# A chunked mLSTM recurrence: norm's first step in front of the decays, chunk loads half a chunk sooner, gated heads' lower parts on GpSimd and heads spread out

## Chip, core and metric

The kernel runs on one NeuronCore of a Trainium2 chip. The metric is the device time of one execution in microseconds (us); a time given for a kernel is the median of several executions. The engines are TensorE (PE, with its weight loads listed apart as PEld), VectorE (DVE), ScalarE (ACT), GpSimd (POOL) and SyncE (SP). PE writes to PSUM banks, which DVE or ACT have to read before the bank can be used again. DMAs are issued here from the queues of SP and POOL. Each engine works through its own queue in order and waits at an instruction until the semaphores it names are reached.

## The reference, cut

The whole program is one inference step of a two-layer decoder: an mLSTM layer, then an attention layer, each followed by a SwiGLU feed-forward part. The change lies in the first layer, in the recurrence over chunks of tokens and the gating behind it:

```python
def mlstm_chunk(state, inp):
    C, n, m = state
    q, k, v, li, lf = inp
    b = jnp.cumsum(lf, axis=-1)
    dmat = jnp.where(causal, b[..., :, None] - b[..., None, :] + li[..., None, :], -jnp.inf)
    m_t = jnp.maximum(inter, jnp.max(dmat, axis=-1))
    s = jnp.einsum('bhtk,bhsk->bhts', q, k) * jnp.exp(dmat - m_t[..., None])
    num = w_inter[..., None] * jnp.einsum('bhtk,bhkv->bhtv', q, C) + jnp.einsum('bhts,bhsv->bhtv', s, v)
    h = num / jnp.maximum(jnp.abs(den), jnp.exp(-m_t))[..., None]
    ...
    C_new = w_c[..., None, None] * C + jnp.einsum('bhs,bhsk,bhsv->bhkv', w_g, k, v)

h = rmsnorm(h, mh_g)                       # over each head's 128 values
out = (h.reshape(B, T, HV) * jax.nn.sigmoid(og)) @ w_out
```

There are 8 heads with 64 key and 128 value columns, 1024 prompt tokens, 16 meta tokens, and 64 sample tokens (8 rows of 8). All data are float32.

## The kernel before

**Tokens.** The 1104 tokens are cut into nine chunks: chunk 0 has the 64 sample and 16 meta tokens, chunks 1 to 8 have 128 each. Three groups `t` of three chunks (`GRP`) make up 336, 384 and 384 columns. Float32 matmuls are made of three products of a rounded high part and a low part (`xh`, `xl`, `whi`, `wlo`): lines L206, L207 and L208. The low part is the value minus its high part.

**The recurrence** (`recurrence`) goes over the chunks; the order of PE, DVE, ACT and POOL in it is the order in which the Python code issues instructions. For chunk `i` it does the following.
- `chunk_load` (four DMAs on POOL's queue: queries and keys `qk`, the decay exponents `eb` as a broadcast, the carry weights `wb` in two halves). The tiles come from three sets, so the load of chunk i + 3 reuses those of chunk i.
- `decay_steps`: eight DVE instructions on `eb`, one a head (L1381), and one exponential on ACT (L1384).
- `chunk_scores`: the products of queries and keys on PE (`sps`, L1398), multiplied into `eb` on DVE (L1400).
- `chunk_keys`: the keys turned (`kps`, L1415) and weighted (`kw` L1417, `wb` L1419).
- `chunk_state`: the new state `C` (PE L1448, DVE L1452, and a multiply on POOL, L1455).
- `chunk_out`: two halves z = 0 and 1 of four heads, each with products with the values (`nps`, L1521) and with the state (L1488); DVE copies the denominators (`den`, L1472), ACT the values (L1480). ACT then makes the exponential of the chunk after next and squares the heads (L1542); in chunks 7 and 8 DVE squares every other head (L1539).

**Filling.** Between these, `f(n)` issues n steps of another job, the matmuls for the output gates (`gates_out`, L206 to L208 into `mmA`): 24 pieces, each eight steps of three matmuls into one of two PSUM banks. ACT empties a bank with a sigmoid into one of three staging tiles `stg` (L994), and POOL stores that to DRAM as `ogD` (L995). The exponential, the root and the sigmoid need different function tables on ACT, and a change shows as ACT_TABLE_LOAD.

**Norm.** After chunks 2, 5 and 8, `norm_heads` normalizes the group's three chunks. Its first step is five small DVE instructions (L1601 to L1605) and a root on ACT (L1606). Its next steps are a reciprocal, a multiply, and one large multiply on DVE for each chunk (L1608 to L1612). For the first two groups these steps are issued inside the next chunk: `next(norm, None)` in `after`, which runs between the two halves of `chunk_out`. So they fall into chunks 3 and 6.

**Heads.** From chunk 7 on the gate job is nearly at its end, and `g` gates finished heads in place of it: five in chunk 7 and five in chunk 8. For a head, `gate_head` turns three chunks' values on PE into a bank `ghps` that it shares with `mmA` (L1628). DVE multiplies it with gain and gate in place of the gate tile (`ogqk`, `ogeb`, L1629). Then `split` rounds to the high part `xh` on ACT (L284) and subtracts for the low part `xl` on DVE (L285). The gate columns are loaded from `ogD` by POOL (L1010) into places made of old `qk` and `eb` tiles; a place is reused once its head is done. The remaining heads are gated later, in the output projection, with other tiles (`ogc`).

**Behind it.** The output projection (`pops`, `mlp`) takes its weights, split already, from DRAM as `wo<-woD`, in pairs of a high and a low half on SP's queue (L547). They go into memory that the recurrence's pools leave, so each pair waits for what used that memory last. POOL loads the residual columns `vA<-hD` (L506).

Of the kernel before, what the change touches and what calls it, by code (L numbers as in the profile page):

```python
# [8 lines left out]
F32 = mybir.dt.float32  # L9
# [19 lines left out]
NT = len(TT)  # L29
# [887 lines left out]
def phase_a(self, vt):  # L917
# [6 lines left out]
    with ExitStack() as c3:  # L924
# [76 lines left out]
        def heads(pp, tag, op=None, some=None):  # L1001
# [11 lines left out]
            def gate(t):  # L1013
                if not left[t]:
                    return False
                while todo and (len(ready) < 3 if callable(op) else op):
                    ahead()
                if t < 0:
                    return False
                og = ready.pop(0)  # L1020
                self.gate_head(t, left[t].pop(0), v, og, pp, tag)
                if not callable(op):

                    used.append(og)
                    if len(used) > 1:
                        op.append(used.pop(0))
                return True
# [161 lines left out]
def recurrence(self, kp, rec, v, qkD, fill, gate):  # L1189
# [15 lines left out]
    with ExitStack() as cr, self.pool("recAp", bufs=2, space=PSUM) as pp:  # L1205
# [28 lines left out]
        with self.pool("rec2") as sets[2], self.pool("rec1", bufs=2) as rp, self.pool("rec3") as sets[0]:  # L1234
# [7 lines left out]
            gate = gate(places)  # L1242
            for i in range(1, NT):
                N2 = load(i + 2) if i + 2 < NT else None
# [13 lines left out]
                def after():  # L1258
                    if i + 1 < NT:
                        self.chunk_keys(i + 1, N, pp, tm)  # L1260
                    if N2:
                        self.chunk_decay(i + 2, N2, tm, cap)
                    next(norm, None)
                    g(2)
                    g(3)
                    g(2)
                    next(norm, None)

                self.chunk_out(i, R, rp, *args, den, ssq, g, exp=N2 and (lambda: N2["exp"]()),
                               then=(lambda: next(state, None)) if i == NT - 1 else None, between=between, after=after)  # L1270
# [18 lines left out]
                R, N = N, N2  # L1289
# [170 lines left out]
def chunk_out(self, i, R, rp, pp, kp, C, v, qkD, eD, wD, tm, den, ssq, f, sp=None, exp=None, then=None, between=None, after=None):  # L1460
# [8 lines left out]
    def done(ps, g, hs):  # L1469
# [21 lines left out]
    if i == 0:  # L1491
        for g, hs in enumerate(((0, 2), (4, 6), (1, 3), (5, 7))):
# [14 lines left out]
            done(ps, g, hs)  # L1507
    else:

        ps = None  # L1510
        for z in range(2):
# [11 lines left out]
            if z:  # L1523
                carried(ps, False)
            for a in range(2):
                done(ps[a], 2 * z + a, (4 * z + a, 4 * z + 2 + a))
            if z == 0:
                after()
        f(2)
# [89 lines left out]
def gate_head(self, t, h, v, og, pp, tag):  # L1619
# [11 lines left out]
    self.split(og[:, :n], yh[:, h, g0:g1], yl[:, h, g0:g1])  # L1631
# [1451 lines left out]
```

## Time and profile before

| | us |
| --- | --- |
| median of 3 runs | 2799.47 |
| lowest, highest run | 2796.45, 2800.47 |
| profiled execution | 2798.37 |
| its span (first to last instruction) | 2796.5 |
| busy: PE, PEld | 2736.1, 2635.6 |
| busy: DVE, ACT, POOL | 1786.7, 1169.0, 848.6 |
| mean granted TensorE clock (1 is full) | 0.996 |

The profile is of one execution. Its totals say which engine is busy; a view in order of time shows for each engine what it ran and what ended the idle time ahead of it; windows give the busy time of each engine and the granted clock in a stretch; a view by line gives the least, median and greatest duration of one kind of instruction. All times on that axis are us from the first instruction. The recurrence takes the stretch from about 215 to 411 us. Busy time of PE is modelled from pipelined matmuls, so 98% is not 98% of its peak.

### The profile page before, as it was taken

The page shows a single profiled execution, that of the slowest core. Times are in us where ns is not written, and L with a number is a line of the kernel's source. Part 1 is how long each engine was busy: PE and PEld are TensorE (multiplying, and loading weights), DVE is VectorE, ACT ScalarE, POOL GpSimd, SP SyncE. Part 2 cuts the span into 40 slices and gives each one's busy share as a digit, 9 for nine tenths or more (in the row PEclk, how much of TensorE's full clock was granted, in tenths as well). Part 3 has the DMA queues.
Part 4 walks back from the last instruction along what each step waited for, and adds up shares of the span by engine and source line. Part 5 has one row for each costly group of instructions (what it writes and reads, how often), then busy time and mean ns, then how long its engine had stood idle before and what let it go on. Part 6 is the DMA issues. An engine that isn't in the chain of part 4 may idle for free. (4 is left out here: it accounts for less than half of the span.)

```text
span 2796.5 us, 60483 instructions
## 1 busy us (share of the span) xinstructions
PE 2736.1 (98%) x23525; PEld 2635.6 (94%) x23525; DVE 1786.7 (64%) x4008; ACT 1169.0 (42%) x2291; POOL 848.6 (30%) x1304
## 2 busy tenths in 40 slices
PE   9999989999999999999999999999999999999998
PEld 8999979999999999999999888777999999999998
DVE  5633556888887666563455443777388888765656
ACT  5432553423323334443444444777343323323345
POOL 3142333133322332124453202544313223323211
PEclk9999999999999999999999999999999999999999
DMA  7666555345554375545453776443524555526556
GB/s 213 176 183 179 152 153 207 105 148 169 166 176 140 117 249 174 188 145 168 139 177 130 246 281 229 158 141 95 150 79 134 175 175 169 162 90 228 185 193 221
DMA packets 432400, 473.05 MB, mean 169 GB/s; under 512 B 37014, under 2 KB 358290, under 8 KB 431090
## 3 DMA queue, kind: packets, MB, share of 16 engines
q1 hardware_dynamic: 380546, 319.98, 37.1%
q0 software_dynamic: 44928, 143.00, 15.6%
q10 hardware_dynamic: 6640, 6.21, 0.7%
q8 instruction: 185, 3.03, 0.5%
q14 instruction: 101, 0.83, 0.1%
HBM read 322.24 MB, written 146.83 MB: 168 GB/s over the span
## 5 line engine op out<-in xcount | busy, mean ns | idle before, releaser
L1685 PE MATMUL m<-xh,slot 128*128 128x276 f32 (+1 forms) x2752 | 539.1, 289 | 2.0 <-ACT fs L1714 2.0
L1685 PEld LDWEIGHTS m<-xh,slot 128*128 128x128 f32 x2752 | 439.1, 188 | 4.4 <-ACT fs L1714 2.6
L1685 PE MATMUL m<-xl,slot 128*128 128x276 f32 (+1 forms) x1376 | 396.7, 288 | 0.0
L1685 PEld LDWEIGHTS m<-xl,slot 128*128 128x128 f32 x1376 | 259.0, 188 | 0.0
L206 PE MATMUL tmps<-slot,xh 128*128 128x256 f32 (+2 forms) x864 | 243.1, 281 | 0.0
L208 PE MATMUL tmps<-slot,xl 128*128 128x256 f32 (+2 forms) x864 | 240.6, 278 | 0.0
L207 PE MATMUL tmps<-slot,xh 128*128 128x256 f32 (+2 forms) x864 | 240.5, 278 | 0.0
L285 DVE TENSOR_TENSOR slot<-slot,slot 128x1024 fp32r<-128x1024 f32 x124 | 162.0, 1307 | 60.1 <-ACT slot L284 58.6
L284 ACT CAST slot<-slot 128x1024 fp32r<-128x1024 f32 x124 | 129.5, 1045 | 142.1 <-PE m L1685 111.4
L207 PEld LDWEIGHTS tmps<-slot,xh 128*128 128x128 f32 (+1 forms) x864 | 159.1, 184 | 0.1
L208 PEld LDWEIGHTS tmps<-slot,xl 128*128 128x128 f32 (+1 forms) x864 | 158.6, 184 | 0.0
L206 PEld LDWEIGHTS tmps<-slot,xh 128*128 128x128 f32 (+1 forms) x864 | 158.4, 183 | 0.2
L206 PE MATMUL mmA<-xh,whi 128*128 128x384 f32 (+1 forms) x384 | 134.2, 349 | 3.8 <-ACT stg L994 3.7
L208 PE MATMUL mmA<-xh,wlo 128*128 128x384 f32 (+1 forms) x384 | 128.4, 334 | 0.0
L207 PE MATMUL mmA<-xl,whi 128*128 128x384 f32 (+1 forms) x384 | 128.4, 334 | 0.0
L285 DVE TENSOR_TENSOR slot<-vA,slot 128x1024 fp32r<-128x1024 f32 (+1 forms) x59 | 82.2, 1396 | 32.7 <-ACT slot L284 31.5
L285 DVE TENSOR_TENSOR slot<-Ht,slot 128x1024 fp32r<-128x1024 f32 (+1 forms) x59 | 82.1, 1394 | 32.7 <-ACT slot L284 31.5
L284 ACT CAST slot<-vA 128x1024 fp32r<-128x1024 f32 (+1 forms) x59 | 60.8, 1035 | 95.5 <-PE m L1685 86.5
L1789 DVE TENSOR_TENSOR ws<-ws 128x128 f32<-128x128 f32 x264 | 94.8, 359 | 8.9
L284 ACT CAST slot<-Ht 128x1024 fp32r<-128x1024 f32 (+1 forms) x59 | 60.8, 1034 | 94.8 <-PE m L1685 86.3
L2905 ACT ACTIVATE s<-s,nb 128x272 f32<-128x272 f32 (+7 forms) x126 | 98.9, 786 | 0.0
L2940 ACT COPY th<-tp 128x768 f32<-128x768 f32 (+1 forms) x80 | 73.5, 920 | 53.8 <-PE tp L2932 30.4
(792 smaller groups left out, 8635.9 us busy)
## 6 DMA issues: line engine op xcount, KB each, us to landing
ws<-in_w_down SPq DMA_DIRECT2D x176, 128.0 KB, 2.7
sD<-ws SPq DMA_DIRECT2D x176, 128.0 KB, 2.0
slot<-sD SPq DMA_DIRECT2D x40, 512.0 KB, 4.2
slot<-in_w_gate_up SPq DMA_DIRECT2D x36, 512.0 KB, 4.0
kp<-in_cache_k SPq DMA_DIRECT2D x32, 512.0 KB, 6.0
vp<-in_cache_v SPq DMA_DIRECT2D x32, 512.0 KB, 6.1
vA<-in_w_gate_up SPq DMA_DIRECT2D x26, 512.0 KB, 4.0
Ht<-in_w_gate_up SPq DMA_DIRECT2D x26, 512.0 KB, 4.0
```

Source lines behind the costliest of these rows:

```text
L206: mm(ps, sh, mh, start=first, stop=False)
L207: mm(ps, sh, ml, start=False, stop=False)
L208: mm(ps, sl, mh, start=False, stop=last)
L284: self.nc.scalar.copy(hi, src)
L285: self.nc.vector.tensor_tensor(out=lo, in0=src, in1=hi.bitcast(F32), op=ALU.subtract)
L1685: nc.tensor.matmul(u.ps[h, b], w[p][:, k], x[q][:, k], start=first and k == i == 0, stop=k == 3 and i == 2, skip_group_check=True)
L1789: tt(out=o, in0=a, in1=b, op=ALU.subtract)
L2905: nc.scalar.activation(ss[z, u], ss[z, u], AF.Exp, bias=nb[:, z : z + 1], accum_out=sm[:, u, z : z + 1])
L2940: nc.scalar.copy(th.rearrange("p x z (u h q) -> p h (x z u) q", h=2, q=64)[:, :, :n], pt[:, :, :n])
```

## The change

It has four parts, all in the recurrence of the first layer:
- In `after`, norm's first step is issued ahead of the decays of chunk i + 2 (it was behind them).
- The load of chunk i + 3 is issued at the end of `chunk_out` of chunk i (`done`), ahead of the last four fill steps. It was issued at the beginning of chunk i + 1, behind those steps. The load of chunk 3 stays in front of the loop.
- `gate_head` takes a flag: the ten heads that are gated within the recurrence have their low part subtracted on POOL instead of DVE. The later heads keep DVE.
- In chunks 7 and 8 the third head moves from between the halves to the second half, between its products with the values and those with the state (`amid`).

```diff
@@ heads / gate
-                self.gate_head(t, left[t].pop(0), v, og, pp, tag)
+                self.gate_head(t, left[t].pop(0), v, og, pp, tag, not callable(op))
@@ recurrence
+            N2 = load(3)
             for i in range(1, NT):
-                N2 = load(i + 2) if i + 2 < NT else None
+                N3 = None
...
                 def after():
                     if i + 1 < NT:
                         self.chunk_keys(i + 1, N, pp, tm)
+                    next(norm, None)
                     if N2:
                         self.chunk_decay(i + 2, N2, tm, cap)
-                    next(norm, None)
                     g(2)
                     g(3)
-                    g(2)
+                    if i < 7:
+                        g(2)
                     next(norm, None)
 
+                def done():
+                    nonlocal N3
+                    if i + 3 < NT:
+                        N3 = load(i + 3)
+
                 self.chunk_out(i, R, rp, *args, den, ssq, g, exp=N2 and (lambda: N2["exp"]()),
-                               then=(lambda: next(state, None)) if i == NT - 1 else None, between=between, after=after)
+                               then=(lambda: next(state, None)) if i == NT - 1 else None, between=between, after=after, done=done,
+                               amid=(lambda: g(3)) if i > 6 else None)
...
-                R, N = N, N2
+                R, N, N2 = N, N2, N3
@@ chunk_out (its inner function done is now called leave)
             if z:
+                if amid:
+                    amid()
                 carried(ps, False)
...
             if z == 0:
                 after()
+        done()
         f(2)
         f(2)
@@ gate_head
-    self.split(og[:, :n], yh[:, h, g0:g1], yl[:, h, g0:g1])
+    hi, lo = yh[:, h, g0:g1], yl[:, h, g0:g1]
+    nc.scalar.copy(hi, og[:, :n])
+    (nc.gpsimd if ahead else nc.vector).tensor_tensor(out=lo, in0=og[:, :n], in1=hi.bitcast(F32), op=ALU.subtract)
```

Below are three places as they stand on the engines; a row is the line, the operation, and out<-in with the shape, and x8 means eight such in a row. Lines of the changed kernel are about ten higher.

DVE in chunk 6, before: `rd` and `fA` are norm's small tiles, and the eight instructions on `eb` are the decays of chunk 8.

```order
L1417 TENSOR_TENSOR kw_4338<-kps_4547,tmA 128x512
L1419 TENSOR_TENSOR wb_4337<-qk_4336,wb_4337 128x512
L1381 SCALAR_TENSOR_TENSOR eb_4486<-eb_4486,tmA,cap 128x128 x8
L1601 SCALAR_TENSOR_TENSOR rd_4562<-den 128x24
L1602 TENSOR_TENSOR rd_4562<-rd_4562,tmA 128x24
L1603 RECIPROCAL rd_4562<-rd_4562 128x24
L1604 TENSOR_TENSOR fA_4563<-ssqA,rd_4562 128x24
L1605 TENSOR_TENSOR fA_4563<-fA_4563,rd_4562 128x24
L1608 RECIPROCAL fA_4563<-fA_4563 128x24
```

The same place with the change:

```order
L1425 TENSOR_TENSOR kw_4300<-kps_4547,tmA 128x512
L1427 TENSOR_TENSOR wb_4299<-qk_4298,wb_4299 128x512
L1612 SCALAR_TENSOR_TENSOR rd_4554<-den 128x24
L1613 TENSOR_TENSOR rd_4554<-rd_4554,tmA 128x24
L1614 RECIPROCAL rd_4554<-rd_4554 128x24
L1615 TENSOR_TENSOR fA_4555<-ssqA,rd_4554 128x24
L1616 TENSOR_TENSOR fA_4555<-fA_4555,rd_4554 128x24
L1389 SCALAR_TENSOR_TENSOR eb_4453<-eb_4453,tmA,cap 128x128 x8
L1619 RECIPROCAL fA_4555<-fA_4555 128x24
```

The decays have moved between norm's first five instructions and its reciprocal, which waits for ACT's root.

POOL from chunk 5 to chunk 6, before: the last load of the loop, that of chunk 8, with the stores of gate columns around it.

```order
L995 DMA ogD<-stg_4416 128x384
L995 DMA ogD<-stg_4458 128x384
L1328 DMA qk_4485<-qkD 128x8x128
L1327 DMA eb_4486<-eD 128x8x128
L1332 DMA wb_4487<-wD 64x4x128 x2
L1455 TENSOR_TENSOR C_107<-C_105,wcP 128x516
```

The same place with the change:

```order
L995 DMA ogD<-stg_4416 128x384
L1336 DMA qk_4452<-qkD 128x8x128
L1335 DMA eb_4453<-eD 128x8x128
L1340 DMA wb_4454<-wD 64x4x128 x2
L995 DMA ogD<-stg_4466 128x384
L1463 TENSOR_TENSOR C_107<-C_105,wcP 128x516
```

The load has passed one store, which now stands behind the load's four DMAs.

POOL in chunks 7 and 8, before: all that stands behind the last multiply of the state is DMAs (reloads of gate columns, the state's store, the last gate store, the residual's load).

```order
L1455 TENSOR_TENSOR C_107<-C_106,wcP 128x516
L1010 DMA ogqk_4647<-ogD 128x336 x2
L1010 DMA ogeb_4648<-ogD 128x336 x2
L1010 DMA ogqk_4782<-ogD 128x384 x2
L1302 DMA out_p_C<-C_105 64x4x128 x2
L995 DMA ogD<-stg_4820 128x384
L506 DMA vA<-hD 128x8x276
```

With the change, from the third head's low part on:

```order
L1644 TENSOR_TENSOR xl<-ogeb_4648,xh 128x336
L1010 DMA ogqk_4647<-ogD 128x336
L1644 TENSOR_TENSOR xl<-ogeb_4648,xh 128x336
L1010 DMA ogeb_4648<-ogD 128x336
L1644 TENSOR_TENSOR xl<-ogqk_4647,xh 128x336
L1010 DMA ogeb_4648<-ogD 128x336
L1010 DMA ogqk_4782<-ogD 128x384 x2
L1310 DMA out_p_C<-C_105 64x4x128 x2
L995 DMA ogD<-stg_4820 128x384
L1644 TENSOR_TENSOR xl<-ogqk_4647,xh 128x336
L1644 TENSOR_TENSOR xl<-ogeb_4648,xh 128x336
L506 DMA vA<-hD 128x8x276
```

Each reload of a gate place now has a subtract in front of it, and the last gate store and the residual's load stand between subtracts. DVE's queue is ten subtracts shorter in the same stretch. On ACT nothing moves.

More of the change, by code (lines that the diff above doesn't have):

```diff
@@ L1459, in chunk_out @@
 @_add(Net)
-def chunk_out(self, i, R, rp, pp, kp, C, v, qkD, eD, wD, tm, den, ssq, f, sp=None, exp=None, then=None, between=None, after=None):
+def chunk_out(self, i, R, rp, pp, kp, C, v, qkD, eD, wD, tm, den, ssq, f, sp=None, exp=None, then=None, between=None, after=None, done=None, amid=None):
     nc = self.nc
@@ L1467, in chunk_out, with leave @@
     nps = []
-    def done(ps, g, hs):
+    def leave(ps, g, hs):
         hx = slice(hs[0], hs[0] + 3, 2)
@@ L1506, in chunk_out @@
                     nc.tensor.matmul(o, qm[:, j * T0 : (j + 1) * T0], R["C0"][:, j, h, :], start=False, stop=(j == 3))
-            done(ps, g, hs)
+            leave(ps, g, hs)
     else:
@@ L1523, in chunk_out @@
             if z:
+                if amid:
+                    amid()
                 carried(ps, False)
             for a in range(2):
-                done(ps[a], 2 * z + a, (4 * z + a, 4 * z + 2 + a))
+                leave(ps[a], 2 * z + a, (4 * z + a, 4 * z + 2 + a))
             if z == 0:
                 after()
+        done()
         f(2)
@@ L1618, in gate_head @@
 @_add(Net)
-def gate_head(self, t, h, v, og, pp, tag):
+def gate_head(self, t, h, v, og, pp, tag, ahead):
     nc = self.nc
```

## The prediction

> **What bounds the kernel now.** I read the page's totals first, then the waits of each engine inside the recurrence (about 215 to 411 us), then the order of time there, engine by engine.
>
> ```profile
> PE 2736.1 (98%) x23525; PEld 2635.6 (94%) x23525; DVE 1786.7 (64%) x4008; ACT 1169.0 (42%) x2291; POOL 848.6 (30%) x1304
> ```
>
> PE is busy for 2736 of 2796.5 us, so any edit that leaves PE's work alone, as this one does (order and engines change, no matmul comes or goes), can only win PE's idle time and time at a lower clock. Here is all of PE's idle time that the edit could reach, by the view in order of time; a row is start, duration, engine, line, operation, out<-in, and in brackets the idle time ahead of it with what ended it.
>
> ```profile
> 338.82 0.44 PE L206 MATMUL mmA<-xh,whi 128*128 128x384 f32 x1 [0.70 <-ACT stg L994]
> ...
> 380.41 0.34 PE L208 MATMUL mmA<-xh,wlo 128*128 128x384 f32 x1
> 383.76 0.69 PE L206 MATMUL mmA<-xh,whi 128*128 128x384 f32 x1 [3.01 <-ACT stg L994]
> 384.25 0.52 PE L207 MATMUL mmA<-xl,whi 128*128 128x384 f32 x1
> 384.57 0.52 PE L208 MATMUL mmA<-xh,wlo 128*128 128x384 f32 x1
> ...
> 388.41 0.52 PE L208 MATMUL mmA<-xh,wlo 128*128 128x384 f32 x1
> 388.86 1.42 PE L1398 MATMUL sps<-qk 64*128 64x128 f32 x16
> 390.11 0.61 PE L1488 MATMUL nps<-C,wb 64*128 64x129 f32 x8
> ...
> 396.29 0.48 PE L1628 MATMUL ghps<-ident,vA 80*128 80x80 f32 x3 [1.66 <-DVE ogqk L1629]
> 397.73 0.51 PE L1628 MATMUL ghps<-ident,vA 80*128 80x80 f32 x3 [0.95 <-DVE ogqk L1629]
> ...
> 400.91 0.51 PE L1628 MATMUL ghps<-ident,vA 80*128 80x80 f32 x3 [0.69 <-DVE ogeb L1629]
> ...
> 406.18 0.51 PE L1628 MATMUL ghps<-ident,vA 80*128 80x80 f32 x3 [1.17 <-DVE ogqk L1629]
> 408.12 0.51 PE L1628 MATMUL ghps<-ident,vA 80*128 80x80 f32 x3 [1.43 <-ACT stg L994]
> ...
> 411.44 0.38 PE L206 MATMUL pops<-xh,wo 128*128 128x276 f32 x1
> ...
> 415.73 0.40 PE L206 MATMUL pops<-xh,wo 128*128 128x276 f32 x1 [0.98 <-DVE noP L1309]
> ```
>
> Three places: 0.70 us in chunk 3, 3.01 us in chunk 6, and some 6 us in pieces where heads are gated in chunks 7 and 8. The 3.01 us cost more than themselves: behind them the same matmul takes 0.52 us instead of 0.34 and starts every 0.32 us. The windows say why.
>
> ```profile
> 384.00:386.00 2.00, 2.00 (x7) 2.00 (x8) 2.00 (x2) 1.98 (x4) 1.40 (x3) 0.50 0.23 86
> 390.00:392.00 2.00, 2.00 (x32) 1.70 (x29) 1.62 (x4) 0.00 (x0) 0.00 (x0) 1.00 0.05 12
> ```
>
> The column behind the five engines' busy times is the granted clock: half speed after the gap, full again at 390. Gaps of up to 1.66 us, in the rows above, brought no such drop.
>
> The Trainium skill's page "TensorE: Matmul & The Clock Gate", section "What's actually happening", puts the drop at an idle window of about 3.4 us; by it a 3.01 us gap might have kept full speed and would be worth 3.0 us only. The trace shows the drop behind 3.01 us, so the measurement decides.
>
> **Norm's first step ahead of the decays (chunks 3 and 6).** What held PE in chunk 6 is seen on DVE, ACT and POOL.
>
> ```profile
> 374.95 0.68 DVE L1419 TENSOR_TENSOR wb<-qk,wb 128x512 f32<-128x512 f32 x1
> 378.25 2.19 DVE L1381 SCALAR_TENSOR_TENSOR eb<-eb,tmA,cap 128x128 f32<-128x128 f32 x8 [2.62 <-DMA eb<-eD]
> 380.36 0.18 DVE L1601 SCALAR_TENSOR_TENSOR rd<-den 128x24 f32<-128x24 f32 x1
> ...
> 381.63 0.31 ACT L1606 ACTIVATE fA<-fA,eps 128x24 f32<-128x24 f32 x1 [5.86 <-DVE fA L1605]
> 381.97 1.28 ACT L994 ACT_TABLE_LOAD   x1
> 383.26 0.45 ACT L994 ACTIVATE stg<-mmA 128x336 f32<-128x336 f32 x1
> ```
>
> DVE waits 2.62 us for the chunk's decay exponents, spends 2.19 us on eight decays, then 1.25 us on norm's five small steps; only then can ACT take the root, change its table (1.28 us) and empty the PSUM bank (0.45 us) that PE waits for. The queue is in order, so the evacuation is late because the root is. With norm's five steps in front they start when `wb` ends, at 375.6, and end at 376.9; the root ends at 377.2, the table at 378.5, the bank is free at 379.0. PE asks for it at 380.75. So the gap goes with 1.7 us to spare, whatever the decays' load does. In chunk 3 the same step moves the root 2.2 us earlier against 0.70 us of idle.
>
> Worth: chunk 3, **0.7 us**. Chunk 6: 3.01 us of idle; the 15 matmuls from 383.76 to the scores at 388.86 take 5.10 us, at 0.174 us each they take 2.61, so 2.5 us; the scores up to 390.11 take 1.25 us where 1.00 is usual at full clock, so 0.25 us. **5.7 us** in all. The decays end 1.25 us later than they would in the old order; their exp is wanted at the next scores' multiply, which in the new order comes at about 384.5, just when the exp ends (root 377.2, evacuations to 382.2, table and exp 2.3 us). That is a tie, but PE is not behind it for another chunk.
>
> **Loads half a chunk sooner.** POOL issued the load behind a store that waits for ACT; the last row is the view of DMA issues, with the size and the time to landing.
>
> ```profile
> 367.80 0.56 POOL L995 DMA_DIRECT2D ogD<-stg  x1 [4.37 <-ACT stg L994]
> ...
> 369.41 0.90 POOL L1327 DMA_DIRECT2D eb<-eD  x1
> 365.02 0.71 PE L1488 MATMUL nps<-C,wb 64*128 64x129 f32 x8
> eb<-eD POOLq DMA_DIRECT2D x1, 512.0 KB, 8.8
> ```
>
> Now it waits only for the chunk's last reader on PE (365.73), so `eb`, behind the issue of `qk` (taken as long as its own 0.90), is issued near 366.7 instead of 369.4 and lands, 8.8 us on, at 375.5 rather than 378.2, ahead of the decays' new place at 376.9. I count it as nothing on top: the norm no longer sits behind it. What it is moved past is the store of gate columns, which now leaves POOL about 1 us later (three DMA issues, 3 us, in front); three staging buffers stand between it and ACT's next write, so this is free as well. Without that cover it is under 1 us a chunk.
>
> **Heads.** Ten heads are gated here. Each is three transposes, a DVE multiply out of PSUM, an ACT rounding and a DVE subtract. The rows with x32, x12 and x8 group one line's instructions: minimum/median/maximum in ns.
>
> ```profile
> 395.58 0.56 DVE L1629 SCALAR_TENSOR_TENSOR ogqk<-ghps,gain,ogqk 128x336 f32<-128x336 f32 x1
> 396.68 0.51 DVE L285 TENSOR_TENSOR xl<-ogqk,xh 128x336 fp32r<-128x336 f32 x1 [0.54 <-ACT xh L284]
> 397.11 0.56 DVE L1629 SCALAR_TENSOR_TENSOR ogqk<-ghps,gain,ogqk 128x336 f32<-128x336 f32 x1
> ...
> L2983 POOL TENSOR_TENSOR xl<-og,xh x32: 725/732/1589, 1749.6 to 1973.5; 128x256 fp32r<-128x256 f32 x32
> L364 POOL TENSOR_TENSOR sq<-sq x12: 763/783/992, 423.5 to 469.0; 128x276 f32<-128x276 f32 x12
> L1455 POOL TENSOR_TENSOR C<-C,wcP x8: 1047/1050/1897, 244.2 to 392.5; 128x516 f32<-128x516 f32 x8
> ogqk<-ogD POOLq DMA_DIRECT2D x4, 168.0 KB, 2.7
> ```
>
> A head costs DVE 1.53 us (395.58 to 397.11), of which 0.54 is waiting for ACT and 0.43 the subtract. Without the subtract DVE frees the bank after 0.56 us. The first 1.66 us stay (DVE is still at `kw` and `wb`). The third head goes behind four matmuls, so its 0.95 goes; of 0.69, 1.17 and 1.43 about 1.3 goes. POOL's price for 336 columns is in no row: from 732 ns at 256 and 763 at 276 it is an estimated 0.87 us; the other end, the 1.59 us row scaled to 336, is 2.1. I take 0.87, as the median row is the nearest in kind. POOL is then nearly full. The second head's multiply ends near 397.4 and its rounding near 397.9, so its subtract ends at 398.8; only then does POOL issue the reload for head five, which lands 2.7 us later, at 401.5, and holds that head's multiply about as late as the old order does; that is why I don't take all of the 6 us. From there: head five to 402.1, DVE's four squares and the state's add to 404.3, `den`, ACT's copies and table to the last gate bank at 407.1 (408.06 now), head eight at 407.3, two more heads behind it. By these steps the output projection starts about 2.2 us sooner than at 411.44, at 409.25, and the 0.98 us in front of its second unit go too.
>
> But its weights stand in the way.
>
> ```profile
> 408.36 0.57 POOL L995 DMA_DIRECT2D ogD<-stg  x1 [1.46 <-ACT stg L994]
> ogD<-stg POOLq DMA_DIRECT2D x1, 192.0 KB, 4.1
> 412.75 1.02 SPq L547 DMA_DIRECT2D wo<-woD  x2
> 420.05 0.39 PE L208 MATMUL pops<-xh,wo 128*128 128x276 f32 x1 [0.42 <-DMA wo<-woD]
> 424.18 0.40 PE L208 MATMUL pops<-xh,wo 128*128 128x276 f32 x1 [0.48 <-DMA wo<-woD]
> ```
>
> The third pair of weights leaves SP only when the last gate store has landed (408.36 and 4.1 us), since it reuses that memory, and PE already waits 0.42 and 0.48 us for the third and fourth pair. That store waits for ACT's bank, 0.9 us earlier by the steps above, and is issued near 407.3, 1.1 us sooner. So of the 3.2 us only what the weights allow comes through: between 1.1 and 3.2, and I take **1.6 us**, near the row that sets it. Below, POOL late with the eighth head's part could cost 1.5 us; above, 4 us if all went.
>
> The page "GPSIMD Engine Reference" of the Trainium skill, section "Performance versus the Vector engine", has a two-tensor add 1.96 times slower there than on VectorE; 0.51 us times that is an estimate of 1.0 us. The sum by it is the same, since 1.0 is still under the point named below.
>
> **Sum.** 0.7 + 5.7 + 1.6 = 8.0 us. The profiled execution took 2798.37 us (its span 2796.5 and 1.9 around it), so 2790.4; the median of the runs shown is 1.1 above that execution, so I forecast **2791.5**.
>
> **Rivals.** (a) The weights take the whole tail: only 6.4 us, 2793.1. For it speak the two DMA waits, against it that the stores do move. (b) The chunk 6 gap closes only in part, because ACT's chain root, table, evacuation is held by something else (the waits name DVE `fA` alone, which speaks against): if 2 us of it stay and the clock still drops (it did behind 3.01 us, not behind 1.66), only 1 of the 5.7 us is won: 0.7 + 1.0 + 1.6, about 2796. (c) The gain is taken back later, where DMA share is at 1.0 (416 to 428 us): 2799, within noise; PE shows no DMA wait behind 424.18, which speaks against. (d) **Slower**: POOL as the bound. The eighth head's part is behind eight subtracts of p, six reload issues of 0.54, the state's store 1.29, the gate store 0.57 and a load of 0.90, all from 396.7: it ends at 402.7 + 8p, and PE wants it at about 411.9 (the eighth step of the first unit from 409.25, at 0.38 us a step). From p = 1.15 PE waits; from 1.6 the wait is over 3 us, halves the clock again (2.7 us) and eats the gain; at 2.1 it is 7.6 + 2.7 against 6.4 won, so 2803. For it: the C multiply's 1.90 us against 1.05 when DVE streams beside it. Against: the medians.
>
> The same page, section "Specifications", says that POOL shares its SBUF interfaces with VectorE and contends with instructions of two SBUF inputs, which speaks for (d); the 1.90 us row agrees in direction.
>
> **How the numbers follow.** Forecast 0.61 (own range 2788.5 to 2793.5), (a) 0.17, (b) 0.13, (c) 0.05, (d) 0.04. A range of 2788 to 2797 leaves out (c), (d) and the forecast's far end. What a measurement can tell from no change is 0.2%, 5.6 us: faster means under 2793.9. That is nearly all of the forecast and half of (a), 0.71; (b), (c) and the rest are the same, 0.25; (d) is slower, 0.04.
>
> **What would show it.** Right: no idle time over 0.2 us before `mmA` in chunks 3 and 6, clock 1.00 throughout, decays without a DMA wait, head multiplies 0.6 us apart, and the first weight wait of `pops` earlier by 1 to 3 us but longer than 0.42. Wrong: POOL subtracts over 1.2 us, `pops` waiting for POOL, a half-clock stretch left, or a new DMA wait behind 424.

## The result, and the profile after

The changed kernel takes 2792.04 us (median of 20 runs, 2788.15 to 2798.47) against 2798.11 us of the kernel before (median of 20 runs, 2796.37 to 2804.12): a ratio of 0.9977, 95% interval 0.9971 to 0.9983. That is some 6 us less; forecast were 8.0 us less than the profiled execution of before and a time of 2791.5 us. Three executions among those behind the table further down, of 4.4 to 7.3 ms, are left out of its ratios.

One warning ahead of the traces. The execution that was profiled after the change is the longest of its 20, 2798.47 us with a span of 2796.9, so the totals of the two profiles must not be subtracted. I measure from the recurrence's first scores to places behind them instead. These are the first scores of before and of after, PE in order of time:

```profile
229.91 0.80 PE L1398 MATMUL sps<-qk 64*80 64x80 f32 x16
```

```profile
232.14 0.80 PE L1406 MATMUL sps<-qk 64*80 64x80 f32 x16
```

**Chunk 6 went as forecast.** DVE and ACT after the change, in order of time:

```profile
376.70 0.18 DVE L1612 SCALAR_TENSOR_TENSOR rd<-den 128x24 f32<-128x24 f32 x1
...
377.86 2.19 DVE L1389 SCALAR_TENSOR_TENSOR eb<-eb,tmA,cap 128x128 f32<-128x128 f32 x8
377.98 0.32 ACT L1617 ACTIVATE fA<-fA,eps 128x24 f32<-128x24 f32 x1 [1.05 <-DVE fA L1616]
378.31 1.28 ACT L994 ACT_TABLE_LOAD   x1
379.60 0.45 ACT L994 ACTIVATE stg<-mmA 128x336 f32<-128x336 f32 x1
```

Norm's five small steps run ahead of the decays, the root follows at 377.98, and the bank is free at 380.05, before PE asks for it. The decays' row has no DMA wait any more. No row of PE from 330 to 386 us shows idle time, chunk 3's among them, and the windows there show full clock (last columns: granted clock, DMA share, GB/s):

```profile
376.00:384.00 8.00, 8.00 (x53) 7.76 (x52) 7.72 (x22) 5.13 (x8) 1.43 (x3) 1.00 0.09 34
384.00:386.00 2.00, 2.00 (x28) 1.65 (x26) 0.39 (x2) 1.99 (x8) 1.87 (x4) 1.00 0.66 209
```

**The end of the recurrence did not.** PE after the change, all its waits over 0.2 us from there to the fifth weights (`slot`):

```profile
391.65 0.48 PE L1639 MATMUL ghps<-ident,vA 80*128 80x80 f32 x3 [1.66 <-DVE ogqk L1640]
395.14 0.51 PE L1639 MATMUL ghps<-ident,vA 80*128 80x80 f32 x3 [0.66 <-DVE ogeb L1640]
400.87 0.51 PE L1639 MATMUL ghps<-ident,vA 80*128 80x80 f32 x3 [1.62 <-DVE ogqk L1640]
...
404.26 0.37 PE L206 MATMUL pops<-xh,wo 128*128 128x276 f32 x1
407.63 0.39 PE L207 MATMUL pops<-xl,wo 128*128 128x276 f32 x1 [0.32 <-POOL xl L1644]
414.38 0.39 PE L206 MATMUL pops<-xh,wo 128*128 128x276 f32 x1 [2.84 <-DMA wo<-woD]
416.36 0.60 PE L208 MATMUL pops<-xh,wo 128*128 128x276 f32 x1 [1.47 <-DMA wo<-woD]
425.65 0.37 PE L206 MATMUL pops<-xh,slot 128*128 128x276 f32 x1
```

The output projection begins 172.1 us after the first scores (404.26 less 232.14) where it was 181.5. But its third unit (the products with the third pair of weights) then waits 2.84 us for the high half of its weights and 1.47 us for the low half, where before it waited 0.42. And a half-clock stretch, gone from chunk 6, has come back here:

```profile
412.24:415.65 3.41, 0.52 (x2) 0.30 (x2) 3.41 (x4) 0.00 (x0) 0.00 (x0) 1.00 0.99 369
415.65:419.06 3.41, 2.70 (x12) 2.70 (x12) 1.96 (x5) 1.27 (x3) 0.77 (x1) 0.50 1.04 410
419.06:422.47 3.41, 3.41 (x17) 3.41 (x17) 0.45 (x2) 0.17 (x1) 0.56 (x1) 0.50 1.02 406
422.47:425.88 3.41, 3.41 (x29) 3.41 (x29) 1.45 (x3) 0.78 (x2) 1.33 (x2) 1.00 1.03 405
```

The same matmuls run 17 to a window at half clock and 29 at full. So of the 9.4 us that the projection starts sooner, the first `slot` matmul keeps 3.9: it stands 193.5 us behind the first scores, 197.4 before.

The weights are bound to the last gate store, as the prediction had it. POOL, SP and DVE after the change:

```profile
403.41 0.57 POOL L995 DMA_DIRECT2D ogD<-stg  x1 [1.71 <-ACT xh L1643]
403.96 2.32 DVE L1612 SCALAR_TENSOR_TENSOR rd<-den 128x24 f32<-128x24 f32 x1
403.99 0.92 POOL L1644 TENSOR_TENSOR xl<-ogqk,xh 128x336 fp32r<-128x336 f32 x1
408.61 1.76 SPq L547 DMA_DIRECT2D wo<-woD  x4
```

The third pair leaves SP at 408.61, when the store has landed. POOL's eight subtracts of 336 columns take 0.90 to 0.92 us (0.87 was estimated), the two of 384 columns 1.02. One thing is new: a DVE instruction of 0.17 us takes 2.32 beside them.

### The profile page after: what moved, and what is told of

It is laid out like the page before. It is cut to its first block, busy times and chain, and to the rows that moved or that the text cites. A ratio compares the mean times of both kernels' runs of the same rounds, so it can differ in the third digit from the quotient of the medians.

```text
span 2796.9 us, 60488 instructions
## 1 busy us (share of the span) xinstructions
PE 2738.6 (98%) x23525; PEld 2638.8 (94%) x23525; DVE 1786.0 (64%) x3998; ACT 1169.4 (42%) x2291; POOL 857.2 (31%) x1314
```

## Experiments

The theory to test, called A: norm's move makes the gain; the heads' part brings the projection forward, but only into the wait for the third weights, and a wait of that length costs the half clock on top. The rival is the prediction's own term: the heads are worth 1.1 to 3.2 us. The table has for each the median, the ratio to the kernel before as it ran beside it (medians 2798.1 to 2798.8), and from its one profiled execution: the first `pops` and the first `slot` matmul, in us behind the first scores, and the windows of 3.41 us at half clock from 380 to 430 us.

| kernel | median us | ratio, 95% interval | pops | slot | half windows |
| --- | --- | --- | --- | --- | --- |
| before | 2798.11 | | 181.5 | 197.4 | 2 |
| the change | 2792.04 | 0.9977 [0.9971, 0.9983] | 172.1 | 193.5 | 2 |
| the change again (e4) | 2793.56 | 0.9983 [0.9974, 0.9992] | 171.8 | 192.9 | 2 |
| norm only (e1) | 2793.49 | 0.9984 [0.9975, 0.9993] | 175.2 | 189.8 | 1 |
| norm and loads (e2) | 2792.18 | 0.9980 [0.9971, 0.9988] | 174.7 | 189.8 | 0 |
| heads only (e5) | 2796.72 | 0.9993 [0.9984, 1.0002] | 177.4 | 196.0 | 3 |
| change, no spread (e6) | 2791.44 | 0.9977 [0.9967, 0.9988] | 173.0 | 190.1 | 1 |
| change, low part on DVE (e7) | 2791.41 | 0.9972 [0.9962, 0.9982] | 174.6 | 191.5 | 1 |
| change, gates first (e3) | 2791.10 | 0.9977 [0.9968, 0.9986] | 176.6 | 189.9 | 2 |
| gates first, low on DVE (e8) | 2793.49 | 0.9982 [0.9973, 0.9991] | 174.7 | 189.1 | 2 |
| change, PE kept busy (e9) | 2791.47 | 0.9977 [0.9967, 0.9986] | 171.2 | 189.9 | 0 |
| change, high half first (e10) | 2790.52 | 0.9975 [0.9965, 0.9985] | 171.3 | 188.0 | 0 |
| both of these (e11) | 2791.82 | 0.9975 [0.9966, 0.9984] | 172.1 | 190.1 | 0 |
| no spread, high half first (e12) | 2791.26 | 0.9969 [0.9960, 0.9979] | 172.9 | 188.7 | 0 |

Two executions of one kernel differ by some 2 us (standard deviation), so the medians tell the parts apart badly, and the two series of the changed kernel itself are 1.5 us apart. The traces tell them apart better, one stretch at a time.

### Norm alone, norm and loads, the change again

e1 is the kernel before with the two lines of norm exchanged; e2 has the loads as well; e4 is the changed kernel once more beside them.

```diff
 e1, on the kernel before:
                         self.chunk_keys(i + 1, N, pp, tm)
+                    next(norm, None)
                     if N2:
                         self.chunk_decay(i + 2, N2, tm, cap)
-                    next(norm, None)
```

> Only norm's first step is moved ahead of the decays; loads and heads stand as before. Weights theory (the heads' gain is taken by the wait for the third pair of projection weights, which hangs on the last gate store): this edit alone gives the whole of the change, -6.4 us against before (ratio 0.9977), the gap in chunk 6 and its half-clock stretch are gone, and the two weight waits stay at about 0.4 us each. Rival, heads keep their gain: this edit gives clearly less than the change, -3 to -5 us. Second rival, the load has to be early as well (the decays still wait for it and hold the rest of norm): a gap of 1 us or more stays in chunk 6 and the gain is under 4 us.

> Norm's first step and the earlier loads; heads as before (subtract on VectorE, third head between the halves). Weights theory: the same as with norm alone, -6.4 us, within 1 us; the decays of chunk 8 don't wait for their load any more. Rival (loads matter for themselves): 1 to 3 us better than norm alone.

> The changed kernel once more, beside the others, for a profile of an ordinary execution (the profiled one took 2798.5 us where the median is 2792.0). Theory that the half-clock stretch behind the weight waits comes and goes: this profile, if its time is near 2792, has a shorter stretch at half clock around 415 to 423 us than 7.5 us, and the same waits ahead of the projection. Rival (the odd 6 us lie elsewhere): the same stretch, and the difference in another stage.

With norm alone the gaps before `mmA` are gone and `pops` starts 6.35 us sooner (175.18 for 181.53); 6.4 was forecast for chunks 3 and 6. In this run the decays still wait 1.71 us for their load, and PE waits for nothing there: the load need not be early as well. By time it is 2793.49, some 5 us under before. As a number that lies in the range of the rival that the heads keep their gain (3 to 5 us) and not at the 6.4 of the weights theory; what speaks for the theory is that the change itself, run beside it (e4), comes out the same, 2793.56. The loads add nothing that can be told from zero. The stretch at half clock around 415 us is as long in e4 as in the change, 6.8 us, so the rival of that run holds: the 4.5 us between the two profiles lie elsewhere, 1.7 of them ahead of the first scores.

What the heads' part does is seen by putting e2 beside the change. PE in e2, its first scores at 228.02 (the first, third and fifth weights' first products):

```profile
402.70 0.38 PE L206 MATMUL pops<-xh,wo 128*128 128x276 f32 x1
...
410.40 0.37 PE L206 MATMUL pops<-xh,wo 128*128 128x276 f32 x1
410.61 0.28 PE L207 MATMUL pops<-xl,wo 128*128 128x276 f32 x1
411.02 0.39 PE L208 MATMUL pops<-xh,wo 128*128 128x276 f32 x1
...
417.83 0.37 PE L206 MATMUL pops<-xh,slot 128*128 128x276 f32 x1
```

Its third unit starts at 410.40, that is 182.4 behind the first scores, with no idle time ahead of it. With the change it starts at 414.38, which is 182.2, and in e4 182.3: **the same place**. The heads' part brings `pops` 2.6 to 2.9 us forward and in these two profiles all of it is waited for. The third pair leaves SP at about the same place as in e2 (403.98 there): 176.5 and, in e4, 175.9 us behind the first scores for 176.0. From that unit on the change loses: its low half is waited for (1.47 us, in e4 1.06), and 6.8 us run at half clock. So `slot` comes 3.1 to 3.7 us later than in e2. By time the change is not faster than norm and loads alone: 2792.04 and 2793.56 against 2792.18.

### The heads alone

> Of the change only the heads' part is kept (lower parts on POOL, third head moved into the second half); norm and the loads stand as in the kernel before. Theory A (the third pair of weights takes what the heads win): pops starts 2 to 3 us sooner after the recurrence's first scores than the 181.5 us of the kernel before, but the third pair of weights, bound to the last gate store, is no more than 0.5 us sooner; PE waits 2.5 to 3.5 us for it and runs at half clock for 5 to 8 us behind it. Time against the kernel before: -0.5 to +2 us. Theory B (the prediction's term): the heads are worth 1.1 to 3.2 us by themselves, with weight waits under 2 us. The gap of 3 us before mmA in chunk 6 is there under both.

e5 is the changed kernel with norm and loads put back. PE in chunk 6 and at the third unit, its first scores at 229.32:

```profile
381.47 0.69 PE L206 MATMUL mmA<-xh,whi 128*128 128x384 f32 x1 [3.24 <-ACT stg L994]
...
415.36 0.39 PE L206 MATMUL pops<-xh,wo 128*128 128x276 f32 x1 [1.75 <-DMA wo<-woD]
417.27 0.39 PE L208 MATMUL pops<-xh,wo 128*128 128x276 f32 x1 [1.39 <-DMA wo<-woD]
```

Here `pops` starts 4.2 us sooner and `slot` 1.4; two waits of 1.75 and 1.39 us and a half window lie between. The time is 0.9993 of before, 0.9984 to 1.0002: about 1.4 us, which is not told from nothing. That is inside the prediction's 1.1 to 3.2 us, with waits under 2 us as its term has them. Theory A missed: it allowed a gain of 0.5 us at most, waits of 2.5 to 3.5 us and weights no more than 0.5 us sooner, and the low half of the third pair came 2.2 us sooner (187.95 us behind the first scores for 190.14). The interval covers both. So with norm in its old place the heads' part looks more like the prediction's term than like A's.

### Which half of the heads' part

> The changed kernel with the third head back between the halves; the lower parts stay on POOL. Theory A: it is POOL's subtracts that bring pops forward, so pops still starts 2 us or more sooner than with norm and loads alone (171 to 173 us after the first scores, against 174.7), the wait for the third weights stays at 3 us or more with the half clock behind it, and the time is that of the change within 1.5 us. Rival: it is the moved third head that brings pops forward; then pops starts at 174 to 175, the weight wait is under 1.7 us, the clock stays full there, and the time is 1 to 3 us under the change.

> The changed kernel with the lower parts back on DVE; the third head stays in the second half. Theory A: pops starts 173 to 175 us after the first scores, the third weights' wait is under 2 us, no half clock there, and DVE's small instructions (rd, jk) are back at 0.2 to 0.3 us from 2.2 to 2.3; time 1 to 3 us under the change. Rival (the moved head alone brings pops forward): as the change, wait 3 us or more and half clock. If the stretched DVE instructions beside POOL are an accident of order, they stay at 2 us here.

```diff
 e6, on the changed kernel:
-                    if i < 7:
-                        g(2)
+                    g(2)
 ...
-                               ... amid=(lambda: g(3)) if i > 6 else None)
 e7, on the changed kernel:
-    (nc.gpsimd if ahead else nc.vector).tensor_tensor(out=lo, ...)
+    nc.vector.tensor_tensor(out=lo, ...)
```

POOL's subtracts alone (e6) bring `pops` 1.7 us forward of e2, the moved head alone (e7) 0.1 us; together 2.6 to 2.9. Neither half by itself runs into the long wait. Both times are 2791.4, 0.6 to 2.1 us under the two medians of the change; the intervals overlap, so a difference is not shown. Theory A had the wait at 3 us or more in e6, and missed: it is 0.99 and 0.86 us. These two rows are PE's, the next two are windows of e6:

```profile
410.58 0.39 PE L206 MATMUL pops<-xh,wo 128*128 128x276 f32 x1 [0.99 <-DMA wo<-woD]
411.96 0.39 PE L208 MATMUL pops<-xh,wo 128*128 128x276 f32 x1 [0.86 <-DMA wo<-woD]
```

```profile
409.70:413.11 3.41, 1.67 (x11) 1.45 (x12) 3.41 (x4) 0.00 (x0) 0.00 (x0) 1.00 1.00 386
413.11:416.52 3.41, 3.41 (x17) 3.41 (x17) 1.88 (x5) 1.27 (x3) 1.33 (x2) 0.50 1.01 369
```

Two waits under 1 us, both within one window of 3.41 us, leave PE idle for 1.74 us of it, and the next window is at half clock. So it isn't the length of one gap that decides.

In e7 the DVE instruction that took 2.32 us is short again, and so are DVE's squares (at most 0.295 us, where the changed kernel has one of 2.22):

```profile
405.59 0.17 DVE L1612 SCALAR_TENSOR_TENSOR rd<-den 128x24 f32<-128x24 f32 x1
```

### The weights sooner

> The changed kernel, with the last eight steps of the gate job issued ahead of chunk 7 instead of five ahead, two in chunk 7 and one in chunk 8. The last gate store leaves some 10 us sooner, so the third pair of weights is no longer behind it. Weights theory: the weight waits of 2.8 and 1.5 us shrink under 1 us together, no half-clock stretch is left at the projection, and the time falls by another 4 to 7 us against the changed kernel (about 2786 to 2788). Rival (GpSimd's subtracts or VectorE set the pace there): within 1.5 us of the changed kernel.

> The changed kernel with all steps of the gates issued before chunk 7 (so the last gate store leaves some 15 us sooner and the weights with it) and the lower parts on DVE. Theory A: with the weights out of the way no weight wait over 0.6 us is left behind the recurrence, and without POOL's subtracts the reloads leave POOL sooner; if heads then wait under 2 us each, the clock stays full and the time is 2 to 4 us under the change. Rival: the reloads land late because they share the DMA engines with the weights (5.9 us in place of 2.6), whatever engine subtracts; then a head waits about 3 us, the clock halves there, and the time is that of the change within 1.5 us.

```diff
 e3, on the changed kernel; e8 has the low part on DVE too:
-                    while self.fills < 3 * KT * KT - KT:
+                    while self.fills < 3 * KT * KT:
```

The last gate store then leaves POOL near 385 us instead of 403 and the third pair of weights SP near 390. The wait for it is gone, as A had it. What A had wrong is the gain. DVE and PE in e3:

```profile
396.12 0.57 DVE L1640 SCALAR_TENSOR_TENSOR ogqk<-ghps,gain,ogqk 128x336 f32<-128x336 f32 x1 [5.84 <-DMA ogqk<-ogD]
```

```profile
396.74 0.67 PE L1639 MATMUL ghps<-ident,vA 80*128 80x80 f32 x3 [3.32 <-DVE ogqk L1640]
400.05 2.09 PE L1529 MATMUL nps<-vA,eb 128*128 128x129 f32 x8 [2.65 <-ACT vA L1488]
```

The reload for head five is now under way together with the weights and lands 5.7 us after its issue instead of 2.5; PE waits 3.3 and 2.65 us among the heads, and the half clock comes there. In e8 it takes 4.8 us; DVE waits only 0.5 us for it, since without POOL's subtracts it is issued sooner, but four waits of 0.37 to 1.02 us among the heads still halve the clock, nearer to that run's rival than to A. The times, 2791.10 and 2793.49, are not told from the change's; A had expected 4 to 7 and 2 to 4 us less.

### What the half clock costs

> The changed kernel with twenty needless matmuls (128 x 276, about 0.128 us each, 2.56 us in all) in front of the third unit of the output projection, into the bank that this unit then starts anew; they fill most of the wait of 2.84 to 3.26 us for the third weights and compute nothing that is used. Theory A (the wait costs its own length and a half-clock stretch of 6.8 us behind it, which comes when about half of a 3.41 us window is idle): the waits there fall to 0.3 to 0.8 us and 1.1 to 1.5 us, the clock is 1.00 there or one 3.41 us stretch is left, and the time is 1.5 to 3 us under the change (2792.7 on average): 2790 to 2791. Rival (the half clock there costs nothing, since PE is bound to the weights' arrival anyway): the stretch goes and the time stays within 0.8 us of the change.

```diff
 e9, on the changed kernel, in the output projection:
+                        if heads and (t, m) == (0, 2):
+                            for k in range(20):
+                                nc.tensor.matmul(ps[:, :SL], ws[1][0][:, k % KT], self.X[0][0][:, k % KT], start=True, stop=True)
                         self.fm_cols(ps[:, :SL], *ws[m], self.X[t])
```

The needless products fill the wait; nothing of them is used. PE's remaining weight waits in e9 and its first `slot` (first scores at 229.09), and the window there:

```profile
411.16 0.40 PE L208 MATMUL pops<-xh,wo 128*128 128x276 f32 x1 [0.27 <-DMA wo<-woD]
415.85 0.39 PE L208 MATMUL pops<-xh,wo 128*128 128x276 f32 x1 [1.02 <-DMA wo<-woD]
419.00 0.37 PE L206 MATMUL pops<-xh,slot 128*128 128x276 f32 x1
```

```profile
410.00:415.00 5.00, 4.56 (x35) 4.11 (x33) 3.84 (x6) 1.27 (x3) 0.78 (x1) 1.00 0.99 362
```

The clock stays full, and `slot` is at 189.9 instead of 192.9 and 193.5. Not all of these 3.0 to 3.6 us are the clock's. The low half of the third weights also came 2.0 to 2.2 us sooner in this execution (182.1 behind the first scores for 184.1 and 184.2), which the edit is not known to cause. The clock's own part is read from that low product to the first `slot` matmul. The rows of e4, its first scores at 230.45:

```profile
414.53 0.60 PE L208 MATMUL pops<-xh,wo 128*128 128x276 f32 x1 [1.06 <-DMA wo<-woD]
...
423.34 0.37 PE L206 MATMUL pops<-xh,slot 128*128 128x276 f32 x1
```

This stretch takes 8.8 us in e4 and 9.3 in the change (416.36 to 425.65). At full clock it takes 6.8 us: in e2 (411.02 to 417.83), and in e9 without its wait of 1.02. So the half clock cost 2.0 and 2.5 us by itself, and the rival (PE is bound to the weights anyway, so that the clock there costs nothing) falls by the trace. By time e9 is 2791.47, 0.6 and 2.1 under the two medians of the change, just outside the 2790 to 2791 that A expected and too little to show alone.

### Another order of the products

> The changed kernel with the third and fourth unit of the output projection reordered: the 16 products with the high half of the weights first, then the 8 with the low half, which lands 2 us later. Theory A: the wait of 1.1 to 1.5 us for the low half goes, that of 2.8 to 3.3 us for the high half stays and still halves the clock; time 0.5 to 1.5 us under the change. Rival: the fourth pair's wait grows by what is won, and the time stays.

> Both edits at once on the changed kernel: twenty needless matmuls in front of the third unit, and high products first in the third and fourth. Theory A: no half clock from 385 to 430 us, one weight wait of under 1 us, the first use of slot 188 to 191 us behind the first scores (192.9 and 193.5 with the change, 189.8 with norm and loads alone), time 2 to 4 us under the change: 2789 to 2790.5. Rival: PE is bound to the weights' arrival; slot's first use stays at 191.5 or later.

> The changed kernel with the third head back between the halves (run before: 2791.4) and the high products first in the third and fourth unit. Theory A: the waits there were 0.99 us for the high half and 0.86 us for the low half in one 3.41 us window; without the second the window is idle for 1 us only, so the clock stays full; time 0.5 to 2 us under the same kernel without the reorder: 2789.5 to 2791. Rival: the waits move to the fourth pair and the time stays at 2791.4.

```diff
 e10 on the changed kernel, e12 on e6; e11 has the products of e9 too:
-                    if not heads and (t, m) == (0, 0):
+                    if (t, m) in (((0, 2), (0, 3)) if heads else ((0, 0),)):
```

In the third and fourth unit the 16 products with the high half go first, and the low half, which lands up to 2 us later, isn't waited for. PE in e10 (first scores at 229.74):

```profile
410.50 0.39 PE L567 MATMUL pops<-xh,wo 128*128 128x276 f32 x1 [1.70 <-DMA wo<-woD]
417.77 0.37 PE L206 MATMUL pops<-xh,slot 128*128 128x276 f32 x1
```

One wait is left of the two; it is shorter than expected (1.70, not 2.8 to 3.3), since the weights came sooner in this execution (the third unit starts at 180.8), and the clock stays full, which A had not expected. `slot` is at 188.0, the earliest of all kernels. But then PE waits for the `slot` weights themselves:

```profile
418.99 0.39 PE L208 MATMUL pops<-xh,slot 128*128 128x276 f32 x1 [0.72 <-DMA slot<-woD]
427.08 0.39 PE L208 MATMUL pops<-xh,slot 128*128 128x276 f32 x1 [0.77 <-DMA slot<-woD]
```

By the end of the projection the lead is gone. The first matmul behind it (`nps<-ones,sq`, L378) stands, behind the first scores, at 207.3 us in e10, 207.2 in e9, 207.7 in e12, 207.8 in e11 and 207.4 in e6, against 207.0 in e1 and 207.5 in e2; the change is at 210.8, e4 at 210.2, before at 214.7. So in these profiles the heads' part brings nothing there over norm alone, in either order of the products, and the change without these edits is some 3 us late.

e12 reaches `slot` at 188.7, with waits of 1.35 and 0.64 us in different windows and full clock; its time, 2791.26, is within 0.2 us of e6's, as the rival had it and not A (0.5 to 2 us less). In e11 the two edits don't add: 190.1 at full clock, as A had it, but with two waits (0.73 and 0.48 us), and the time, 2791.82, is above what A expected. e12 has the lowest ratio of all, 0.9969 (0.9960 to 0.9979), and e10 the lowest median, 2790.52, below what A expected. Both are under the change by 0.8 to 3 us of median, with intervals that overlap.

## Why the prediction was right, and where it was not

The time came out 0.5 us above the forecast. Part of this nearness is luck: the forecast stood on a median of three runs of before, 2799.47, where twenty gave 2798.11. The gain is 6.1 us (4.8 to 8.1 by the interval) for the 8.0 forecast. By its steps:

- **Norm ahead of the decays (6.4 us): right, mechanism and size.** The chain root, table, evacuation is freed as described, and `pops` starts 6.35 us sooner with norm alone. By time e1 is 4.9 us under before; the rest up to 6.4 is within its interval (2.0 to 7.0 us).
- **Loads counted as nothing: not contradicted.** The decays' DMA wait is gone, and e1 and e2 can't be told apart.
- **POOL's price: right; the point from which PE waits: too high.** 0.90 to 0.92 us for 0.87, under the 1.15 from which rival (d) has PE wait. PE waited for POOL all the same, 0.32 us, which the prediction listed as a sign against it: the sum behind the 1.15 has POOL work without a pause, and POOL waited for ACT, 1.71 us of it in front of the last gate store. It is a small part of what followed, and the change is not slower.
- **Heads worth 1.6 us: the term that failed.** The prediction said "of the 3.2 us only what the weights allow comes through". The bringing forward was right (2.6 to 2.9 us in the trace, and head five was held by its reload as foretold), and rival (a), the weights taking all of it, is what the two profiles of the change show: the third unit starts at 182.2 to 182.4 with the heads' part and without. In e10, whose code is the same up to there, it starts at 180.8, so the weights' arrival differs by 1.5 us between executions; behind the projection nothing of that is left either. The prediction made the last gate store 1.1 us sooner and the weights with it; the store is 0.1 to 1.1 us sooner (170.9 to 171.3 behind the first scores, 171.4 and 172.0 in e1 and e2), and its slower landing (4.9 us for 4.1 before and 3.7 in e2) ate that.
- **What was left out: the wait for the weights costs more than its length.** The prediction counted 3.01 us in chunk 6 as idle time and half clock, and so did rival (d) with a wait for POOL, but a wait that grows at the third unit (2.84 us in the trace) has no half clock in its sum. By its own reading of chunk 6 such a wait brings it, and it cost 2.0 and 2.5 us. In the trace the heads are therefore a loss of 3.1 to 3.7 us at `slot` on top of norm and loads; by time between a loss of 1.4 and a gain of 0.1, and alone a gain of 1.4 us with an interval that includes nothing. Their sign is left open; that they bring the forecast 1.6 us on top of norm is not seen in any run.
- **"Clock 1.00 throughout": wrong**, for this reason. **"Head multiplies 0.6 us apart": wrong** as well. The first four start at 390.94, 392.17, 393.35 and 394.52, 1.2 us apart, since DVE waits up to 0.67 us for PE's transposes. The first weight wait is longer than 0.42 us, as foretold, and sooner, but by 7.9 us instead of 1 to 3 (182.2 behind the first scores for 190.1), mostly norm's doing.

The total came out near because norm's part is nearly the whole of it; the likeliest case was, by the steps, rival (a) with its 2793.1, and the two medians of the change lie on both sides of that.

## To carry to other kernels

Before work ahead of a stage is speeded up, look at what that stage waits for next: where a transfer sets its start, the gain turns into a wait, and on PE a wait can cost a half-clock stretch as well. In the traces here a wait was cheaper when it was split over the program, covered with products that don't need the late half, or filled with needless ones; none of these got further than leaving the earlier work as it was (e1, e2), and by time none was told from the change. Where an engine queue empties a bank behind a chain of small steps (here five DVE steps and a root), moving that chain in front of the long work is worth the gap and the half clock behind it.

## What the runs showed of the hardware

**The half clock goes by windows.** Read in steps of 0.1 us, every stretch at half clock between 150 and 2770 us lasts 3.41 or 6.83 us, and in one execution all begin on one grid: before at 167.56, 246.06, 382.60 and 1570.43, each a whole number of 3.413 us from the others. The windows of before on that grid:

```profile
379.19:382.60 3.41, 1.56 (x12) 1.11 (x8) 2.75 (x13) 0.95 (x2) 0.00 (x0) 1.00 0.00 0
382.60:386.01 3.41, 2.25 (x7) 2.25 (x8) 3.41 (x5) 3.23 (x6) 1.41 (x3) 0.50 0.14 53
386.01:389.43 3.42, 3.42 (x14) 2.98 (x14) 0.15 (x1) 3.41 (x18) 1.90 (x4) 0.50 0.70 218
389.43:392.84 3.41, 3.41 (x46) 3.11 (x43) 1.95 (x4) 0.18 (x2) 0.36 (x1) 1.00 0.13 48
392.84:396.25 3.41, 1.79 (x16) 1.55 (x15) 2.08 (x5) 0.82 (x3) 0.69 (x1) 1.00 0.00 0
```

A window with PE idle for 1.85 us halves the next one; the last row has 1.62 us of idle time, and the clock after it stays full. Over the 14 profiles, every window on its grid with 2.0 us of idle time or more was followed by half clock; from 1.46 to 1.95 us it went either way. A window already at half clock was followed by another after less, 0.71 to 1.17 us of idle time (before, the change, e4, e5 and e8, from 380 to 430 us). The grid lies elsewhere against the program in each execution, so one and the same gap can cost a window or none: PE waits 2.4 to 3.0 us near 1562 us (before `ktp`) in all 14 profiles, and a window at half clock follows in nine. The gap in chunk 6 cost two in both profiles that have it (before and e5). A window at half clock costs 1.7 us at most; two cost 2.5 us in the change's projection. From 150 to 2770 us the profiled execution of the change has seven such windows, that of e2 two, so these make at most 8.5 of the 9.1 us between their spans (2796.9 and 2787.8). The runs on record agree that this is a large part of why executions of one kernel differ: of those of the kernel before beside the experiments, the 31 with a mean clock of 0.997 took 2796.7 us on average, the 15 with 0.995 took 2800.8. The prediction's mark, "not behind 1.66", was true of single gaps and not a rule: e6 shows 0.99 and 0.86 us doing it together. The Trainium skill's page "TensorE: Matmul & The Clock Gate", section "What's actually happening", has a free-running window of 4096 cycles, 3413 ns; the grid agrees to 0.02 us. Its condition for the drop, an idle window, is stricter than what is seen here: some half a window is enough.

Idle time as the profile shows it is not all that counts. In e7 a window with 1.46 us of it, full of small transposes, was followed by half clock. So is, in 11 profiles, a window near 165 us with 0.2 us or less, and in seven one near 1745 or 1780 us with 0.73 to 1.03. The windows of e7:

```profile
391.87:395.28 3.41, 1.95 (x20) 1.42 (x22) 2.33 (x7) 1.49 (x4) 1.22 (x3) 1.00 0.43 132
395.28:398.69 3.41, 3.41 (x23) 3.07 (x20) 2.56 (x15) 2.13 (x10) 1.59 (x4) 0.50 0.55 169
```

What does count there was not tried.

**Small DVE instructions beside POOL's subtracts.** The last `rd<-den` takes 0.17 or 0.18 us with the subtract on DVE (before, e1, e2, e7, e8) and 0.69 to 2.41 us in all nine profiles with it on POOL, where it runs beside one; one of DVE's squares takes up to 2.2 us there. The Trainium skill's page "GPSIMD Engine Reference", section "Specifications", says that the two share their SBUF interfaces and contend where DVE reads two SBUF inputs; the rows agree that there is contention. In the change's trace PE waits for none of it.
